# PSUM banks split by user, RWKV operands computed in PSUM, and the recurrence's old state added by products with the identity

## The chip, the cores and the metric

The kernel runs on one core of a Trainium2 chip. The metric is the device time of one execution in microseconds; the median of several runs is compared. The engines are TensorE (PE, with its weight loads PEld), VectorE (DVE), ScalarE (ACT), GpSimd (POOL) and SyncE (SP), which issues the DMAs. PSUM has eight banks of 512 float32 values on 128 partitions.

## The reference

One trunk layer over 256 context tokens and 2048 latent tokens, width 1024. The input is normalised and modulated, then projected once to all the columns that three mixers need: a chunkwise mLSTM (6 heads of 64), an RWKV-7 recurrence (6 heads of 64, two directions) and an RG-LRU (256 channels). The mixers' gated outputs are concatenated and projected back. The part of the reference that the change is about is the RWKV recurrence, one step per token:

```
def rwkv_step(S, inp):
    r, w, kh, b, kt, v = inp
    Sk = einsum('bhvk,bhk->bhv', S, kh)
    S = S * w[:, :, None, :] - Sk[..., None] * b[:, :, None, :] + v[..., None] * kt[:, :, None, :]
    return S, einsum('bhvk,bhk->bhv', S, r)
```

with `w = exp(-DECAY * sigmoid(w0 + tanh(wl) @ w2))` and `b`, `kt` built from `a = sigmoid(a0 + al @ a2)`.

## The kernel before

The kernel is one long program. A planner on the host (class Flow) decides the order of TensorE's instructions alone: processes written as generators issue products and then yield how long they would wait, or an Event; Flow advances a model clock by a cost for each product, serves the process of lowest rank that is ready, and lets the dense projection (rank 9) fill the gaps. Flow knows nothing of PSUM banks. The order on the other engines is chosen by the tile framework, which also inserts the semaphores; `high_priority` pulls an instruction forward there. A PSUM tile is one bank, and a tile that is asked for waits until a bank of its pool is released by its last reader.

The stages, with their time in the trace: modulation and gates (0 to 100 us), the dense projection with the token shift (to 637), **derive** (637 to 1045), the mLSTM (to 1378), and the **chains** (forward to 1729, backward to 2017), with a tail to 2058. The dense projection goes on beside derive and the mLSTM; partial output products (`po`, function out_part) run beside the forward chains, and the final output (`pz`, `yT`, function out_last) beside the backward chains.

PSUM before the change: one pool `ps` of eight banks with one tag, from which every stage and every dense product takes.

**derive** makes the operands of the recurrence, in 54 blocks of 256 tokens (of one head pair `p` and one direction `d`), grouped in seven stages of six or eight blocks. `block()`: four products put the decay and the gate into the bank `pw`; ScalarE's tanh brings both into the SBUF tile `KB` (L950, L952); VectorE makes the sigmoid of the decay (L955) and its running sum (L956, a scan); ScalarE takes two exponentials (E at L957, cs at L958) and one of two scaled gates (L960), VectorE the other (L959); four VectorE products (L965, L967, L969 or L971, L972) make the operands, which DMAs store to DRAM. `worker()`: some 11 us of Flow's time later eight small products fill the bank `pt` from KB, and six ScalarE copies bring its parts to `DG` and `OF` (L1007 to L1009). When all blocks of a stage are there, VectorE transposes DG (L1049) and GpSimd inverts the triangles in 60 small operations (L1058, L1060); `merge()` finishes with products pY and pX.

**chains** runs the recurrence for three head pairs at once, as three processes, each with 36 steps of 64 tokens forward and 36 backward. `prepare` makes the operands of two steps (banks `ga`, `gb`; L1592, L1595, L1598). A step uses one bank `cq`, cut in four parts of 64 columns, `qk`, `yy`, `pp`, `ps`, with a product for each of the two heads on its half of the partitions:

1. `qk` and the first part of `yy` from the old state (eight passes on TensorE, `cq<-cg`; a float32 product is two passes);
2. ScalarE: `q = -qk` (L1630), and GpSimd: `sd` = old state times the decay `Dk` (L1635);
3. `pp` from q; two copies of pp into the place of the state, both on VectorE forward (L1644) or both on ScalarE backward (L1642);
4. `ps` (`cq<-cg,bt`) and the second part of `yy` (`cq<-cg,G`);
5. VectorE, once for each head: new state = ps times Dk plus sd (L1659); yy is copied by ScalarE forward (L1667) or added by VectorE backward (L1665).

A step yields WAIT of 1.38, 0.9 and 1.28 us of Flow's time between its parts, or LONG while the RG-LRU isn't done.

Of the kernel before, what the change touches and what calls it, by code (L numbers as in the profile page):

```python
# [228 lines left out]
def tile_hymba(ctx, tc, I, O):  # L229
# [64 lines left out]
    X["sh_open"] = Event()  # L294
    X["ps"] = ctx.enter_context(tc.tile_pool(name="ps", bufs=8, space=PSUM))
# [16 lines left out]
def side(X, ctx):  # L312

    F, tc = X["F"], X["tc"]
    yield from build_h(X)
    yield X["done"][_GATES]
    with tc.tile_pool(name="gr", bufs=1, side="right") as gr:
        rows = Event()
        F.spawn(gate_rows(X, gr, rows), 2)
        with tc.tile_pool(name="mg", bufs=1, side="right") as mg:  # L320

            gt = [mg.tile([128, T], F32, name=n) for n in ("gt", "RA", "RB")]
            for i, g in enumerate(gt):
                X["nc"].gpsimd.memset(g, 0.0)
                for q in range(4):
                    X["nc"].sync.dma_start(g[32 * q:32 * q + 6], X["U"][_GATES][32 * i + 6 * q:32 * i + 6 * q + 6])
            for g in gt[1:]:
                X["nc"].vector.tensor_tensor(out=gt[0], in0=gt[0], in1=g, op=ALU.add)
            yield 15000.0
            yield from gates(X, mg, *gt)  # L330
        if rows.t is None:
            yield rows
    with tc.tile_pool(name="sh", bufs=1, side="right") as sh:
        shift_setup(X, sh)
        F.fire(X["sh_open"])
        lru_in = Event()
        F.spawn(lru_gates(X, sh, lru_in), 2)
        for n in _SEQ2:
            yield X["done"][n]
            yield from shift_post(X, sh, n)  # L340
            F.fire(X["post"][n], 0.0)
        if lru_in.t is None:
            yield lru_in
# [12 lines left out]
def late(X, ctx):  # L356
# [4 lines left out]
    X["last"], X["parted"] = Event(), Event()  # L361
# [163 lines left out]
def projector(X):  # L525
# [45 lines left out]
    group = [pick(), pick()]  # L571
    with X["tc"].tile_pool(name="w0", bufs=1, side="left") as w0:
# [5 lines left out]
        ps = {(n, b): X["ps"].tile([56 if n == _GATES else 128, 512], F32, tag="b", name=f"pp_{n}_{b}") for n in group for b in (1, 0)}  # L578
# [13 lines left out]
        for b, (t0, n) in list(enumerate(BLOCKS))[2:]:  # L592
            if X["hb"][b].t is None or X["hb"][b].t > F.now:
                yield X["hb"][b]
            ps = X["ps"].tile([56, 512], F32, tag="b", name=f"pp_{_GATES}_{b}")
# [12 lines left out]
            ps = X["ps"].tile([128, 512], F32, tag="b", name=f"pp_{name}_{b}")  # L608
# [5 lines left out]
    while nxt:  # L614
# [8 lines left out]
        for b in (1, 0, 2, 3, 4):  # L623
# [6 lines left out]
            ps = X["ps"].tile([128, 512], F32, tag="b", name=f"pp_{name}_{b}")  # L630
# [202 lines left out]
def derive(X, dv):  # L833
# [13 lines left out]
    Es = []  # L847
    for i in range(2):
        Es.append(dv.tile([128, 4, 65], F32, name=f"E{i}"))
        nc.gpsimd.memset(Es[i][:, :, 0:1], 1.0)  # L850
# [24 lines left out]
    ahead, cnt = [], [0]  # L875
# [21 lines left out]
    def merge(sid, XT, g, end):  # L897
# [4 lines left out]
        pY = X["ps"].tile([128, 16, 32], F32, tag="b", name=f"pY{sid}{g}")  # L902
# [8 lines left out]
        pX = X["ps"].tile([128, 16, 32], F32, tag="b", name=f"pX{sid}{g}")  # L911
# [17 lines left out]
    def block():  # L929

        _, sid, p, d, i0, l0, nm, wa, z = ahead.pop(0)
        E = Es[cnt[0] % 2]
        cnt[0] += 1
        bw = d == 1
        pw = X["ps"].tile([128, 2, 256], F32, tag="b", name=f"pw{nm}")
# [11 lines left out]
        sa = KB[:, :, 0]  # L947
        sw = KB[:, :, 1]
# [15 lines left out]
        k = KB[:, :, 2:4]  # L964
        nc.vector.tensor_tensor(out=k, in0=k, in1=z4, op=ALU.mult)  # L965
        kh, r3 = tok(z[:, 0]), z[:, 1].rearrange("p (c j) -> p c j", j=64)
        nc.vector.tensor_tensor(out=KB[:, :, 1], in0=E[:, :, 0:64], in1=kh, op=ALU.mult)  # L967
        if bw:
            nc.vector.tensor_tensor(out=KB[:, :, 0], in0=E[:, :, 64:0:-1], in1=r3[:, ::-1], op=ALU.mult)  # L969
        else:  # L970
            nc.vector.tensor_tensor(out=KB[:, :, 0], in0=E[:, :, 1:65], in1=r3, op=ALU.mult)  # L971
# [751 lines left out]
def out_part(X, ou, W):  # L1723
# [16 lines left out]
    while nxt:  # L1740
        t, parts = nxt
        o = ou.tile([128, D], F32, tag="o", name=f"o{t}", bufs=3)
        for n in range(2):
# [3 lines left out]
            if n == 0:  # L1747
                nxt = load()
# [222 lines left out]
```

## Time and profile before

| what | value |
| --- | --- |
| median of 3 runs | 2064.82 us (2057.7 to 2073.31) |
| the profiled execution | 2059.59 us |
| its span, first to last instruction | 2057.9 us |
| PE busy over the span | 1801.6 us (88%) |
| DVE, ACT, POOL busy | 1367.0 (66%), 977.6 (48%), 795.0 us (39%) |
| mean granted TensorE clock | 0.933 of full speed |

Busy time is an average over stages with different limits, so it is read stage by stage. The granted clock is the share of full speed that TensorE was given in a stretch. An engine waits in order: what stands behind a waiting instruction waits too.

### The profile page before, as it was taken

The page shows a single profiled execution, that of the slowest core. Times are in us where ns is not written, and L with a number is a line of the kernel's source. Part 1 is how long each engine was busy: PE and PEld are TensorE (multiplying, and loading weights), DVE is VectorE, ACT ScalarE, POOL GpSimd, SP SyncE. Part 2 cuts the span into 40 slices and gives each one's busy share as a digit, 9 for nine tenths or more (in the row PEclk, how much of TensorE's full clock was granted, in tenths as well). Part 3 has the DMA queues.
Part 4 walks back from the last instruction along what each step waited for, and adds up shares of the span by engine and source line. Part 5 has one row for each costly group of instructions (what it writes and reads, how often), then busy time and mean ns, then how long its engine had stood idle before and what let it go on. Part 6 is the DMA issues. An engine that isn't in the chain of part 4 may idle for free. (4 is left out here: it accounts for less than half of the span.)

```text
span 2057.9 us, 46221 instructions
## 1 busy us (share of the span) xinstructions
PE 1801.6 (88%) x16648; PEld 1201.0 (58%) x16778; DVE 1367.0 (66%) x3271; ACT 977.6 (48%) x2634; POOL 795.0 (39%) x1200
## 2 busy tenths in 40 slices
PE   5899999999999878788899798878778788999996
PEld 3555655656666556555566565555555556777774
DVE  3747366777643898998324766647885576777774
ACT  5732446565434667776242545542332233444442
POOL 0210011112110688888722444342653232444442
PEclk9899999999999988889999899989888999999997
DMA  7343344564548778887254666645986545576662
GB/s 284 118 142 90 126 123 133 153 168 148 132 127 247 215 207 223 225 214 176 80 154 135 188 171 170 171 118 154 292 268 193 164 136 149 163 196 203 197 190 72
DMA packets 353370, 350.60 MB, mean 170 GB/s; under 512 B 109554, under 2 KB 294978, under 8 KB 350728
## 3 DMA queue, kind: packets, MB, share of 16 engines
q1 hardware_dynamic: 353142, 347.65, 59.2%
q8 instruction: 133, 2.18, 0.5%
q14 instruction: 95, 0.78, 0.1%
HBM read 211.18 MB, written 136.37 MB: 169 GB/s over the span
## 5 line engine op out<-in xcount | busy, mean ns | idle before, releaser
L1635 POOL TENSOR_SCALAR sd<-cg,Dall 128x128 f32<-128x128 f32 x210 | 135.8, 654 | 267.1 <-DVE cg L1659 164.0
L1659 DVE SCALAR_TENSOR_TENSOR cg<-cq,Dall,sd 64x64 f32<-64x64 f32 x408 | 114.5, 281 | 46.4 <-PE cq L168 36.6
L1060 POOL TENSOR_TENSOR W<-W,tmp 128x30 f32<-128x30 f32 (+14 forms) x210 | 139.0, 662 | 16.1
L1058 POOL TENSOR_TENSOR tmp<-W 128x30 f32<-128x30 f32 (+14 forms) x210 | 133.0, 633 | 15.9
L168 PE MATMUL cq<-cg,bt 128*64 128x64 f32 x840 | 68.5, 246 | 49.7 <-DVE cg L1644 44.6
L1283 ACT ACTIVATE nb<-nb,aT 128x128 f32<-128x128 f32 x216 | 71.6, 393 | 82.5 <-DMA nb<-nm_d 72.4
L168 PE MATMUL cq<-cg 128*64 128x64 f32 x1728 | 92.9, 230 | 8.2 <-DVE cg L1659 8.2
L168 PEld LDWEIGHTS cq<-cg,bt 128*64 128x64 f32 x840 | 44.1, 142 | 84.9 <-DVE cg L1644 54.8
L168 PE MATMUL ga<-cg 64*64 64x128 f32 (+1 forms) x864 | 76.9, 270 | 16.9 <-DMA cg<-ch 16.9
L1630 ACT ACTIVATE q<-cq 128x64 f32<-128x64 f32 x216 | 45.5, 223 | 95.7 <-PE cq L168 92.3
L1592 DVE TENSOR_TENSOR cg<-gb,rmask 64x256 f32<-64x256 f32 x108 | 44.7, 413 | 66.3 <-PE gb L168 61.1
L168 PEld LDWEIGHTS cq<-cg 128*64 128x64 f32 x1728 | 72.9, 141 | 24.3 <-issue 9.5
L168 PE MATMUL pz<-owhi,zhi 128*128 128x512 f32 x180 | 82.1, 456 | 4.5 <-ACT zhi L1822 4.5
L1598 ACT ACTIVATE bt<-ga 128x256 f32<-128x256 f32 x108 | 41.3, 383 | 87.0 <-DVE G L1595 83.4
L168 PE MATMUL pt<-KB 64*64 64x64 f32 x864 | 41.9, 244 | 45.7 <-DVE KB L972 45.6
L1284 POOL TENSOR_SCALAR_AFFINE_SELECT nb<-nb 128x256 f32<-128x256 f32 x108 | 44.8, 421 | 93.0 <-ACT nb L1283 63.6
L168 PE MATMUL gb<-cg 64*64 64x128 f32 (+1 forms) x864 | 75.7, 270 | 0.9 <-DMA cg<-ch 0.9
L168 PE MATMUL pz<-owhi,zlo 128*128 128x512 f32 x180 | 73.5, 409 | 3.3 <-DVE zlo L1823 3.3
L168 PE MATMUL pz<-owlo,zhi 128*128 128x512 f32 x180 | 72.9, 405 | 0.0
L168 PEld LDWEIGHTS ga<-cg 64*64 64x64 f32 x864 | 48.2, 142 | 41.9 <-issue 27.9
L168 PE MATMUL cq<-q,cg 128*64 128x64 f32 x864 | 59.4, 236 | 9.9 <-ACT q L1630 9.9
L168 PE MATMUL pp_v<-hhi,whi_v 128*128 128x512 f32 (+1 forms) x120 | 67.4, 562 | 0.3 <-ACT whi_v L514 0.3
(511 smaller groups left out, 6180.0 us busy)
## 6 DMA issues: line engine op xcount, KB each, us to landing
cg<-ch SPq DMA_DIRECT2D x216, 192.0 KB
wa<-wa SPq DMA_DIRECT2D x54, 256.0 KB
z<-z SPq DMA_DIRECT2D x27, 512.0 KB
ch<-KB SPq DMA_DIRECT2D x108, 128.0 KB
ch<-KB SPq DMA_DIRECT2D x54, 256.0 KB
nb<-nm_d SPq DMA_DIRECT2D x108, 128.0 KB
lr<-L SPq DMA_DIRECT2D x16, 768.0 KB
lL<-lr SPq DMA_DIRECT2D x16, 768.0 KB
```

The lines of the kernel that those rows point to most:

```text
L168: self.nc.tensor.matmul(out, lhsT, rhs, start=start, stop=stop, **kw)
L1058: nc.gpsimd.tensor_tensor(out=tv, in0=W[:, j + 1:32, j:j + 1].to_broadcast([128, m, j]), in1=W[:, j:j + 1, 0:j].to_broadcast([128, m, j]), ...
L1060: nc.gpsimd.tensor_tensor(out=W[:, j + 1:32, 0:j], in0=W[:, j + 1:32, 0:j], in1=tv, op=ALU.add)
L1283: nc.scalar.activation(nb[:, d, j], nb[:, d, j], AF.Exp, bias=aT[:, c, d, 2 * p + j:2 * p + j + 1])
L1284: nc.gpsimd.affine_select(out=nb[:, d], in_=nb[:, d], pattern=[[0, 2], [1 - 2 * d, 128]], base=0, channel_multiplier=-1 + 2 * d, compare_o ...
L1592: nc.vector.tensor_tensor(out=cg[o, :, RK[h]], in0=src[o], in1=mask[o, d].rearrange("p a c -> p (a c)")[:, None].to_broadcast([64, 2, 128] ...
L1598: nc.scalar.activation(bt, ga[:, 1], AF.Copy)
L1630: nc.scalar.activation(q, qk, AF.Copy, scale=-1.0)
L1635: nc.gpsimd.tensor_scalar(sd, cg.rearrange("p (n c) -> p n c", c=64)[:, 0::9], Dk, None, op0=ALU.mult)
L1659: nc.vector.scalar_tensor_tensor(out=nxt[h][b], in0=ps[b], scalar=Dk[b], in1=sd[b, 1 - h], op0=ALU.mult, op1=ALU.add)
```

## The change

Banks: two of the eight (`pd`) serve the dense products alone (`pp_`, `po`, `pz`), the other six serve the stage that runs: six of one kind up to the shift and for the mLSTM; for derive two (`m`, pY and pX), three (`c`, pw and the new kb) and one (`b`, pt); for the chains three (`b`: ga, gb, yT) and three (`c`: cq). `po` and `pz` take one of two slots in Flow first.

derive: the decay's sigmoid and its exponential E stay in pw, the sigmoid's affine step goes to ScalarE, both gates are made by ScalarE into a second bank kb, the four VectorE products read PSUM on one side, and the two OF copies of a block go to VectorE.

chains: GpSimd's sd is gone; two products with the identity add the old state into ps, and the new state is ps times Dk, for one head on ScalarE, for the other on VectorE. The two copies of pp are split the same way.

```diff
-    X["ps"] = ctx.enter_context(tc.tile_pool(name="ps", bufs=8, space=PSUM))
+    X["pd"] = ctx.enter_context(tc.tile_pool(name="pd", bufs=2, space=PSUM))
...
+    with tc.tile_pool(name="psa", bufs=6, space=PSUM) as X["ps"]:
...
-    with tc.tile_pool(name="dv", bufs=1, side="right") as dv:
+    with tc.tile_pool(name="dv", bufs=1, side="right") as dv, tc.tile_pool(name="psb", bufs=1, space=PSUM) as X["ps"]:
         yield from derive(X, dv)
-    with tc.tile_pool(name="ml", bufs=1, side="right") as ml:
+    with tc.tile_pool(name="ml", bufs=1, side="right") as ml, tc.tile_pool(name="psm", bufs=6, space=PSUM) as X["ps"]:
         yield from mlstm(X, ml)
...
+    X["ps"] = ctx.enter_context(tc.tile_pool(name="psr", bufs=3, space=PSUM))
     chains(X, ctx.enter_context(tc.tile_pool(name="rc", bufs=1, side="right")))
...
-        pw = X["ps"].tile([128, 2, 256], F32, tag="b", name=f"pw{nm}")
+        pw = X["ps"].tile([128, 2, 256], F32, tag="c", name=f"pw{nm}", bufs=3)
...
-        nc.scalar.activation(sw, pw[:, 0].rearrange("p (c j) -> p c j", j=64), AF.Tanh, scale=0.5, bias=hv[:, i:i + 1])
+        sw, sa = pw[:, 0], pw[:, 1]
+        nc.scalar.activation(sw, sw, AF.Tanh, scale=0.5, bias=hv[:, i:i + 1])
+        nc.scalar.activation(sw, sw, AF.Copy, scale=0.5, bias=0.5)
...
-        nc.scalar.activation(sa, pw[:, 1].rearrange("p (c j) -> p c j", j=64), AF.Tanh, scale=0.5, bias=hv[:, i:i + 1])
+        nc.scalar.activation(sa, sa, AF.Tanh, scale=0.5, bias=hv[:, i:i + 1])
...
-        nc.vector.tensor_scalar(cs, tok(sw), 0.5, 0.5, op0=ALU.mult, op1=ALU.add)
-        nc.vector.tensor_tensor_scan(out=cf, data0=sm, data1=cf, initial=0.0, op0=ALU.mult, op1=ALU.add)
-        nc.scalar.activation(E[:, :, 1:65], cs, AF.Exp, scale=-DECAY)
-        nc.scalar.activation(cs, cs, AF.Exp, scale=DECAY)
-        nc.vector.tensor_scalar(KB[:, :, 2], tok(sa), ab[:, 0, p:p + 1], ab[:, 1, p:p + 1], op0=ALU.mult, op1=ALU.add)
-        nc.scalar.activation(KB[:, :, 3], tok(sa), AF.Identity, scale=ab[:, 2, p:p + 1], bias=ab[:, 3, p:p + 1])
+        nc.vector.tensor_tensor_scan(out=cf, data0=sm, data1=sw[:, ::-1] if bw else sw, initial=0.0, op0=ALU.mult, op1=ALU.add)
+        k = X["ps"].tile([128, 4, 2, 64], F32, tag="c", name=f"kb{nm}", bufs=3)
+        sat = tok(sa)
+        for s in range(2):
+            nc.scalar.activation(k[:, :, s], sat, AF.Identity, scale=ab[:, 2 * s, p:p + 1], bias=ab[:, 2 * s + 1, p:p + 1])
+        E = sw.rearrange("p (c j) -> p c j", j=64)
+        nc.scalar.activation(sw, cf, AF.Exp, scale=-DECAY)
+        nc.scalar.activation(cf, cf, AF.Exp, scale=DECAY)
...
-        nc.vector.tensor_tensor(out=KB[:, :, 1], in0=E[:, :, 0:64], in1=kh, op=ALU.mult)
+        nc.vector.tensor_copy(KB[:, :, 1, 0:1], kh[:, :, 0:1])
+        nc.vector.tensor_tensor(out=KB[:, :, 1, 1:64], in0=E[:, :, 0:63], in1=kh[:, :, 1:64], op=ALU.mult)
...
-        nc.vector.tensor_tensor(out=k, in0=cs[:, :, None].to_broadcast([128, 4, 2, 64]), in1=k, op=ALU.mult)
+        nc.vector.tensor_tensor(out=KB[:, :, 2:4], in0=cs[:, :, None].to_broadcast([128, 4, 2, 64]), in1=k, op=ALU.mult)
...
-                nc.scalar.activation(OF[sid][a:a + 32, ls], pt[a:a + 32, :, 32:64], AF.Copy)
+                nc.vector.tensor_copy(OF[sid][a:a + 32, ls], pt[a:a + 32, :, 32:64])
...
-    parts, slots, pairs = [0] * NT, Slots(F, 4), Slots(F, NP)
+    parts, slots, pairs = [0] * NT, Slots(F, 3), Slots(F, NP)
...
-                with X["tc"].high_priority(offset=HP):
-                    sd = rc.tile([128, 2, 64], F32, tag="sd", name=f"sd{nm}", bufs=3)
-                    nc.gpsimd.tensor_scalar(sd, cg.rearrange("p (n c) -> p n c", c=64)[:, 0::9], Dk, None, op0=ALU.mult)
+                for h, b, o in heads:
+                    F.mm(ps[b], ident[:, b], cg[:, ST[h]], start=False, stop=False, skip_group_check=True)
...
-                    if d:
+                    if h:
                         nc.scalar.activation(cg[b, ST[h]], pp[b], AF.Copy)
...
-                        nc.vector.scalar_tensor_tensor(out=nxt[h][b], in0=ps[b], scalar=Dk[b], in1=sd[b, 1 - h],
-                                                       op0=ALU.mult, op1=ALU.add)
+                    if not last and h:
+                        nc.vector.tensor_scalar(nxt[h][b], ps[b], Dk[b], None, op0=ALU.mult)
+                    elif not last:
+                        nc.scalar.activation(nxt[h][b], ps[b], AF.Copy, scale=Dk[b])
```

## Rows read from the trace of the kernel before

**Rows 1.** Busy time by stretch: PE, PEld, DVE, ACT, POOL, clock, DMA share, GB/s.
```profile
700.00:950.00 250.00, 202.74 (x2349) 141.44 (x2373) 234.09 (x323) 179.29 (x554) 214.16 (x310) 0.85 0.83 218
1378.00:1729.00 351.00, 278.24 (x3580) 196.53 (x3588) 245.93 (x737) 111.27 (x359) 132.66 (x178) 0.89 0.67 195
1550.00:1729.00 179.00, 145.08 (x2055) 104.70 (x2052) 116.75 (x396) 59.57 (x200) 49.44 (x77) 0.92 0.56 161
1757.00:2017.00 260.00, 253.80 (x3492) 186.26 (x3488) 202.06 (x628) 120.77 (x450) 118.36 (x137) 1.00 0.64 186
```

**Rows 2.** Groups by line, VectorE, 637 to 975 us: count | busy us, mean ns | idle before.
```profile
L972 DVE TENSOR_TENSOR KB<-cs,KB 128x512 f32<-128x512 f32 x54 | 48.2, 898 | 3.2 <-ACT cs L958 3.2
L965 DVE TENSOR_TENSOR KB<-KB,z 128x512 f32<-128x512 f32 x54 | 47.4, 880 | 0.1
L956 DVE TENSOR_TENSOR_SCAN cs<-sm,cs 128x256 f32<-128x256 bf16 x54 | 40.8, 755 | 0.1
L959 DVE TENSOR_SCALAR KB<-KB,rab 128x256 f32<-128x256 f32 x54 | 34.4, 637 | 1.1
L967 DVE TENSOR_TENSOR KB<-E,z 128x256 f32<-128x256 f32 x54 | 33.4, 618 | 5.1 <-ACT E L957 5.0
L955 DVE TENSOR_SCALAR cs<-KB 128x256 f32<-128x256 f32 x54 | 25.3, 469 | 17.6 <-ACT KB L950 17.5
L969 DVE TENSOR_TENSOR KB<-E,z 128x256 f32<-128x256 f32 x27 | 18.9, 701 | 0.0
```

**Rows 3.** Groups by line, ScalarE, 637 to 975 us.
```profile
L960 ACT ACTIVATE KB<-KB,rab 128x256 f32<-128x256 f32 x54 | 32.3, 600 | 0.6
L1008 ACT ACTIVATE OF<-pt 32x128 f32<-32x128 f32 x108 | 27.2, 252 | 0.0
L950 ACT ACTIVATE KB<-pw,hv 128x256 f32<-128x256 f32 x54 | 25.5, 473 | 9.3 <-DMA ch<-KB 8.3
```

**Rows 4.** Single tiles and lines, VectorE: ns min/median/max, first and last start.
```profile
L965 DVE TENSOR_TENSOR KB<-KB,z x54: 658/884/1730, 645.8 to 965.2; 128x512 f32<-128x512 f32 x54
...
L1832 DVE TENSOR_TENSOR zo<-pz,zo x36: 678/681/693, 1764.7 to 2049.1; 128x512 f32<-128x512 f32 x36
...
L1592 DVE TENSOR_TENSOR cg<-gb,rmask x108: 374/417/419, 1379.4 to 2002.2; 64x256 f32<-64x256 f32 x108
...
L1595 DVE TENSOR_TENSOR G<-ga,rmask x108: 282/283/283, 1380.5 to 2003.3; 64x128 f32<-64x128 f32 x108
```

**Rows 5.** Line 1049: the transpose that opens each of derive's seven stages.
```profile
L1049 DVE STREAM_TRANSPOSE W<-DG x7: 1916/1996/2076, 680.1 to 972.3; 128x1024 f32<-128x1024 f32 x7
```

**Rows 6.** Line 1667 (yr<-cq, 108 times): its engine sat idle until: us, times.
```profile
  DVE cg L1659: 75.2, 64
```

**Rows 7.** Timeline of the backward half: start us, us, engine, line, operation.
```profile
1864.10 0.20 PEld L168 LDWEIGHTS cq<-cg,G 128*64 128x64 f32 x4
...
1864.21 0.32 PEld L168 LDWEIGHTS cq<-cg 128*64 128x64 f32 x8
1864.27 0.40 PE L168 MATMUL cq<-cg 128*64 128x64 f32 x8
...
1864.78 0.23 ACT L1630 ACTIVATE q<-cq 128x64 f32<-128x64 f32 x1 [1.63 <-PE cq L168]
```

**Rows 8.** Timeline of the forward half, two places.
```profile
1400.84 0.31 PEld L168 LDWEIGHTS cq<-cg 128*64 128x64 f32 x8 [0.23 <-issue]
...
1401.45 0.22 ACT L1630 ACTIVATE q<-cq 128x64 f32<-128x64 f32 x1
...
1691.34 0.48 DVE L1644 COPY cg<-cq 64x64 f32<-64x64 f32 x2 [0.19 <-PE cq L168]
...
1691.87 0.20 PEld L168 LDWEIGHTS cq<-cg,bt 128*64 128x64 f32 x4 [0.58 <-DVE cg L1644]
```

**Rows 9.** The page's costliest groups: sd on GpSimd, the new state on VectorE.
```profile
L1635 POOL TENSOR_SCALAR sd<-cg,Dall 128x128 f32<-128x128 f32 x210 | 135.8, 654 | 267.1 <-DVE cg L1659 164.0
L1659 DVE SCALAR_TENSOR_TENSOR cg<-cq,Dall,sd 64x64 f32<-64x64 f32 x408 | 114.5, 281 | 46.4 <-PE cq L168 36.6
```

More of the change, by code (lines that the diff above doesn't have):

```diff
@@ L293, in tile_hymba @@
     X["hk"] = [Event() for _ in range(NK)]
-    X["sh_open"] = Event()
-    X["ps"] = ctx.enter_context(tc.tile_pool(name="ps", bufs=8, space=PSUM))
+    X["sh_open"], X["open"] = Event(), Event()
+    X["pd"] = ctx.enter_context(tc.tile_pool(name="pd", bufs=2, space=PSUM))
     with ExitStack() as sa:
@@ L314, in side @@
     F, tc = X["F"], X["tc"]
[L315 to L343, printed above, removed]
-    with tc.tile_pool(name="dv", bufs=1, side="right") as dv:
+    with tc.tile_pool(name="psa", bufs=6, space=PSUM) as X["ps"]:
+        F.fire(X["open"])
+        yield from build_h(X)
+        yield X["done"][_GATES]
+        with tc.tile_pool(name="gr", bufs=1, side="right") as gr:
+            rows = Event()
+            F.spawn(gate_rows(X, gr, rows), 2)
+            with tc.tile_pool(name="mg", bufs=1, side="right") as mg:
+                gt = [mg.tile([128, T], F32, name=n) for n in ("gt", "RA", "RB")]
+                for i, g in enumerate(gt):
+                    X["nc"].gpsimd.memset(g, 0.0)
+                    for q in range(4):
+                        X["nc"].sync.dma_start(g[32 * q:32 * q + 6], X["U"][_GATES][32 * i + 6 * q:32 * i + 6 * q + 6])
+                for g in gt[1:]:
+                    X["nc"].vector.tensor_tensor(out=gt[0], in0=gt[0], in1=g, op=ALU.add)
+                yield 15000.0
+                yield from gates(X, mg, *gt)
+            if rows.t is None:
+                yield rows
+        with tc.tile_pool(name="sh", bufs=1, side="right") as sh:
+            shift_setup(X, sh)
+            F.fire(X["sh_open"])
+            lru_in = Event()
+            F.spawn(lru_gates(X, sh, lru_in), 2)
+            for n in _SEQ2:
+                yield X["done"][n]
+                yield from shift_post(X, sh, n)
+                F.fire(X["post"][n], 0.0)
+            if lru_in.t is None:
+                yield lru_in
@@ L360, in late @@
     X["todo"], X["ahead"] = [1, 0] + list(range(NT - 1, 1, -1)), []
-    X["last"], X["parted"] = Event(), Event()
+    X["last"], X["parted"], X["banks"] = Event(), Event(), Slots(F, 2)
     ou = ctx.enter_context(tc.tile_pool(name="ou", bufs=1, side="left"))
@@ L571, in projector @@
     group = [pick(), pick()]
+    yield X["open"]
     with X["tc"].tile_pool(name="w0", bufs=1, side="left") as w0:
@@ L577, in projector @@
         ev = {n: evac(X, n) for n in group}
-        ps = {(n, b): X["ps"].tile([56 if n == _GATES else 128, 512], F32, tag="b", name=f"pp_{n}_{b}") for n in group for b in (1, 0)}
+        ps = {(n, b): X["pd" if n == _GATES else "ps"].tile([128, 512], F32, tag="b", name=f"pp_{n}_{b}")[0:56 if n == _GATES else 128]
+              for n in group for b in (1, 0)}
         for k in range(NK):
@@ L846, in derive @@
         nc.vector.tensor_scalar(ab[off, 2 * s + 1], ka[off], -0.5, 1.0, op0=ALU.mult, op1=ALU.add)
[L847 to L850, printed above, removed]
     CP = TP // 64
@@ L976, in block @@
         nc.sync.dma_start(ch[64:128, :, 2:4], KB[64:128, :, 0:2])
-        nc.scalar.activation(X["Dall"][:, p, d, i0:i0 + per], E[:, :, 64], AF.Copy)
+        nc.scalar.activation(X["Dall"][:, p, d, i0:i0 + per], E[:, :, 63], AF.Copy)
         if d:
@@ L1743, in out_part @@
         for n in range(2):
-            po = X["ps"].tile([128, 512], F32, tag="b", name=f"po{t}{n}")
+            yield from X["banks"].take()
+            po = X["pd"].tile([128, 512], F32, tag="b", name=f"po{t}{n}")
             yield from out_mm(F, po, n, parts, W)
             nc.scalar.activation(o[:, 512 * n:512 * n + 512], po, AF.Copy)
+            X["banks"].give()
             if n == 0:
@@ L1828, in head @@
             ns = slice(512 * n, 512 * n + 512)
-            po = X["ps"].tile([128, 512], F32, tag="b", name=f"pz{t}{n}")
+            yield from X["banks"].take()
+            po = X["pd"].tile([128, 512], F32, tag="b", name=f"pz{t}{n}")
             yield from out_mm(F, po, n, parts, W)
@@ L1835, in head @@
             nc.scalar.activation(po, o[:, ns], AF.Square, accum_out=ss[:, n:n + 1])
+            X["banks"].give()
         nc.vector.tensor_tensor(out=ss[:, 0:1], in0=ss[:, 0:1], in1=ss[:, 1:2], op=ALU.add)
```

26 lines of the change are left out of this document (10 added, 16 removed).

## The prediction

> **What bounds the kernel now.** I read the windows by stage first, then the groups by line of the stage in question, then the timeline of single steps. Three stages are touched by more than the naming of banks.
>
> The stage that prepares the recurrence's operands (derive) is held by VectorE: in 700 to 950 us it is busy for 234 of 250 us, ScalarE for 179, TensorE for 203 at a granted clock of 0.85 [rows 1]. Its pace is the distance of the seven transposes that open a stage of eight blocks: 972.3 - 680.1 = 292.2 us for six, 48.7 us a stage, 6.09 us a block [rows 5]. VectorE's seven operations of a block add up to 0.90 + 0.88 + 0.76 + 0.64 + 0.62 + 0.47 + 0.70 = 4.96 us [rows 2]; transposes and the rest fill what is left.
>
> The forward half of the chains (1378 to 1729 us) is held by no engine: TensorE works 278 of 351 us, so 73 us are idle, at a clock of 0.89 [rows 1]. The backward half with the final output (1757 to 2017) is held by TensorE: 253.8 of 260 us at a clock of 1.00, 6.2 us idle [rows 1]. What is added to TensorE's queue there lengthens the kernel one for one.
>
> **One property of the waits decides this case.** In a forward step ScalarE's copy of yy (L1667) reads columns 64 to 127 of the bank cq; nothing that it needs comes from VectorE, which reads columns 192 to 255 of the same bank at L1659. Yet 64 of 108 copies waited for L1659, 75.2 us in all [rows 6]. So accesses of two engines to one bank are kept in the order of the program, whichever columns they touch. The change puts new work into exactly such places.
>
> **Part 1, the banks of the dense products.** They get two of their own. A bank is written by 24 products of 512 columns. Four passes of 64 columns take 1864.21 - 1864.10 = 0.11 us [rows 7], 0.028 each, so 24 products last over 24 x 8 x 0.028 = 5.4 us, and emptying one takes 0.68 us on VectorE [rows 4] plus about as much on ScalarE before it. The second bank is free long before it is wanted, and TensorE's order is written by the planner, which knows nothing of banks here. I take 0; the ends are -5 us (waits of products for a bank that a stage held) and +10 us (an emptying that stands behind something else).
>
> **Part 2, derive.** Off VectorE go L955 (0.47) and L959 (0.64). The four products keep one operand in SBUF and get one in PSUM. With two SBUF operands L965 took 658 to 1730 ns, median 884; with one in PSUM a VectorE instruction of the same width took 678 to 693 ns although GpSimd was half busy, and those of 256 and 128 columns were as steady at 0.42 and 0.28 [rows 4]. So: scan 0.76, two products of 512 columns 1.36, two of 256 columns 0.84, a copy of four elements at most 0.24 (half of the two copies of 0.48 [rows 8]; I take 0.2), two OF copies 2 x 0.28 = 0.56: 3.72 us instead of 4.96, 1.24 us a block. If VectorE stayed the bound, 48 blocks would give -60 us.
>
> It does not stay alone. ScalarE gets a copy (0.47 by L950) and a second Identity (0.60 by L960) and gives up two OF copies (0.25 each): +0.57 us a block, 41 blocks in 250 us, so 179 + 23 = 202 of 250 us [rows 1, 3]. And by the property above a block becomes one file of hand-overs: three activations on the bank pw, scan, two Identities, two Exp, products, ScalarE's Dall; and the six copies out of pt, which ran in one engine, alternate ScalarE, VectorE, ScalarE, twice. In series: 3 x 0.47 + 0.76 + 2 x 0.60 + 2 x 0.47 (an Exp by L950) + 0.2 + 2 x 0.42 + 0.68 = 6.0 us, and with some ten hand-overs of 0.11 (1864.67 to 1864.78 [rows 7]) about 7. A block takes two banks of three (pw and kb), so one and a half blocks are under way: 7 / 1.5 = 4.7 us a block at the best, against 6.09 now. I take 5.8, since ScalarE now stops twice a block for a VectorE queue that also holds transposes of 2 us [rows 5]: 48 x 0.3 = -15 us. Ends: -60 (VectorE's relief in full) and +20 (54 blocks that lose 0.4 us each to the stops).
>
> **Part 3, the identity products.** Removed: GpSimd's sd, 210 times 0.65 us, and the two-operand form of 408 VectorE instructions [rows 9]. VectorE's and GpSimd's time was not on the path of the backward half. In each pair of halves one copy moves to the other engine; by the order within a bank they follow one another: 0.24 + 0.11 + 0.22 = 0.57 us instead of 0.48 for pp, and about 0.57 instead of 0.56 for the state. That adds 0.1 us to a step's latency, 36 x 0.1 = 4 us where latency counts (forward).
>
> Added: two products a step, four passes, 0.11 us [rows 7]. And a wait: the identity product writes into cq after q's activation has read qk from cq in the program, so TensorE, which has just issued yy, stops until q is read. Queued behind it on TensorE are the other two chains' products, prepare and all dense work, and every engine that waits for those. Backward: the last eight passes begin to issue at 1864.21 and are out at 1864.44; q ends at 1864.78 + 0.23 = 1865.01; TensorE restarts 0.05 us after a release (copies end at 1691.82, weight load at 1691.87 [rows 8]). The stop is 1865.06 - 1864.44 = 0.62 us [rows 7] with ScalarE free. ScalarE is 46% busy there (120.8 of 260 [rows 1]) with pieces of 0.2 to 0.6 us, so I add 0.1: 0.72. For the 105 steps: 75.6 + 105 x 0.11 = 87 us; up to 6 us of it fall into idle time: **+85** (ends 81 and 87).
>
> Forward: issue ends at 1400.84 + 0.23 = 1401.07, q at 1401.45 + 0.22 = 1401.67, restart 1401.72: 0.65 us [rows 8]. 105 x (0.65 + 0.11) = 80 us, against 73 us of idle time. Part of that idle time is a wait for things that come sooner relative to a later TensorE, part is chain latency that stays. I let half be absorbed: 40 + 4 for latency = **+44** (ends: 80 - 73 = 7, and 110, when nothing is absorbed and q stands behind ScalarE's waits for L1659 of 75.2 / 64 = 1.2 us [rows 6]).
>
> Clock: 81% busy went with 0.92 (1550 to 1729), 98% with 1.00 [rows 1]. The backward half would be busy for (254 + 12) / (260 + 80) = 78%; at 0.92 its 266 us of work would cost 23 us more; I take half, **+12**.
>
> The Trainium skill has a rule on this in "PSUM — Partial Sum Buffer", section "PSUM bank collisions raise a hardware error": two engines on one bank must be kept apart by bank and by group of 32 partitions, whatever the columns. That is the wait of the identity product, whose columns and q's lie on the same 128 partitions, and it speaks against the change; with rows 6 the trace agrees. The same section lets different groups of partitions overlap; by that the two halves of 64 partitions could run side by side, and the forward half would come out some 16 us lower than in my sum. No row shows such an overlap.
>
> **Sum.** The profiled execution took 2059.6 us (the median of the three runs is 2064.8, 0.25% above). 2059.6 - 15 + 0 + 44 + 85 + 12 = 2185.6, so **2186 us**, 6% slower.
>
> **Rivals.** (a) Faster: the identity product does not wait, because the order within a bank is kept between reads but a product into other columns may pass. Then the backward half pays only 105 x 0.11 = 12 us, the forward half hides its 12, and derive keeps three quarters of VectorE's relief, -45: 2059.6 + 12 - 45 = 2027. It holds if TensorE starts the identity product within 0.1 us of yy; against it stands the waiting yr copy. (b) Slower by less: derive gets all of the 60 and the forward half absorbs all it can: 2059.6 - 60 + 7 + 81 = 2088. For it: VectorE's 94%. (c) Slower by more: nothing is absorbed, the clock falls, and derive is stopped by its hand-overs: 2059.6 + 20 + 110 + 87 + 23 = 2300. For it: three engines then wait for one another in each step. (d) Nothing to be measured: q is read sooner, because ScalarE has less in front of it, and a stop costs 0.3 us: backward 105 x 0.41 = 43, forward 0, derive -45: 2058.
>
> **How the numbers follow.** My case 0.56, (a) 0.10, (b) 0.15, (c) 0.13, (d) 0.06. A measurement of this kernel tells about 1% from no change; so faster 0.10, same 0.06, slower 0.84. My case by itself runs from about 2130 to 2240; the range reaches to (b) and (c), 2075 to 2300, and leaves out (a), (d) and half of (c).
>
> **What would show it.** Right: among TensorE's waits a large new one of the product cq<-ident or its weight load for ScalarE's q, over 200 times and 0.5 us or more each, some 130 to 160 us in all; in the backward half TensorE's idle time rises from 6 to over 60 us and the stretch from 288 us (1729 to 2017) to about 385; derive's stages still 44 to 49 us apart, VectorE well under 90% there, ScalarE waiting for OF copies. Wrong: identity products that follow yy at once; a backward half under 310 us; stages of derive under 42 us.

## The result, and the profile after

| | before | after |
| --- | --- | --- |
| median of 4 runs | 2064.24 us | 2271.96 us (2265.87 to 2274.33) |
| ratio | | **1.0998**, interval 1.0951 to 1.1046: slower |
| the profiled execution, its span | 2059.59, 2057.9 us | 2265.87, 2264.2 us |

The stages below are the distances between first starts in the traces: of a product into pw, of pk (the mLSTM's first), of ga, of the 109th q (the first backward step), and of the last q. In the trace after they stand at:

```profile
662.00 0.82 PE L168 MATMUL pw<-wa,w20first 128*128 128x256 f32 x4
...
1123.74 0.49 PE L175 MATMUL pk<-ident,vk 128*128 128x128 f32 x3
...
1850.71 0.23 ACT L1633 ACTIVATE q<-cq 128x64 f32<-128x64 f32 x1 [1.18 <-PE cq L168]
```

| stage | before | after | difference | forecast |
| --- | --- | --- | --- | --- |
| up to derive | 637.7 | 662.0 | +24 | 0 (dense banks) |
| derive | 418.7 | 461.7 | +43 | -15 |
| mLSTM | 321.6 | 324.2 | +3 | |
| forward chains | 349.5 | 402.8 | +53 | +44 |
| backward chains | 290.4 | 374.3 | +84 | +85, and +12 for the clock |
| tail | 40.0 | 39.1 | -1 | |

The sum is +206 us. Two thirds of it lie where the forecast had put nearly all; a third lies in two places to which it had given nothing, or a gain.

TensorE's waits, the view of all waits of the kernel after (engine, product, line, who released it: us in total, times, longest):

```profile
PEld cq L168 <- ACT q L1633: 152.6, 211, 3.3
...
PE cq L168 <- ACT q L1633: 122.2, 210, 3.1
...
PE pt L168 <- ACT DG L1012: 80.9, 33, 8.5
```

The first two lines are the forecast wait, seen from the weight loads and from the products: in all 210 steps the identity products stand for q, the loads 152.6 / 211 = 0.72 us each, the products 122.2 / 210 = 0.58 us. The third line was not forecast. The next that matters is in the list for 300 to 722 us, which ends 60 us into derive:

```profile
PE pp_v L168 <- ACT ug L746: 16.9, 4, 9.0
...
PE pp_k L168 <- ACT ug L746: 3.8, 1, 3.8
```

The windows, in the columns of [rows 1]: derive, the forward half, the backward half.

```profile
722.00:972.00 250.00, 192.74 (x2065) 132.38 (x2085) 160.51 (x324) 181.73 (x498) 166.04 (x314) 0.84 0.76 196
1448.00:1851.00 403.00, 311.58 (x3993) 219.47 (x4000) 187.34 (x526) 161.30 (x571) 60.59 (x70) 0.86 0.59 169
1851.00:2225.00 374.00, 311.46 (x4356) 225.64 (x4358) 217.82 (x698) 143.18 (x499) 65.45 (x48) 0.97 0.50 144
```

In the backward half TensorE is idle for 374 - 311.5 = 62.5 us, where [rows 1] had 6. In derive no engine is nearly full any more: VectorE fell from 234 to 161 of 250 us, and yet its stages stand further apart (before in [rows 5], 48.7 us):

```profile
L1052 DVE STREAM_TRANSPOSE W<-DG x7: 1961/1996/2005, 722.2 to 1048.0; 128x1024 f32<-128x1024 f32 x7
```

(1048.0 - 722.2) / 6 = 54.3 us a stage. The single step, from the timeline of the backward half (as [rows 7]):

```profile
1959.81 0.32 PEld L168 LDWEIGHTS cq<-cg 128*64 128x64 f32 x8
...
1959.87 0.40 PE L168 MATMUL cq<-cg 128*64 128x64 f32 x8
...
1960.43 0.20 ACT L1633 ACTIVATE q<-cq 128x64 f32<-128x64 f32 x1
1960.68 0.20 PEld L168 LDWEIGHTS cq<-cg,ident 128*64 128x64 f32 x4 [0.55 <-ACT q L1633]
1960.68 0.34 PE L168 MATMUL cq<-cg,ident 128*64 128x64 f32 x4 [0.41 <-ACT q L1633]
```

The last weight load of the eight products ends at 1960.13, the products are out at 1960.27, q is read from 1960.43 to 1960.63, and only then does the identity product begin, with everything behind it in TensorE's queue.

### The profile page after: what moved, and what is told of

It is laid out like the page before. It is cut to its first block, busy times and chain, and to the rows that moved or that the text cites. A ratio compares the mean times of both kernels' runs of the same rounds, so it can differ in the third digit from the quotient of the medians.

```text
span 2264.2 us, 47168 instructions
## 1 busy us (share of the span) xinstructions
PE 1893.4 (84%) x17487; PEld 1259.4 (56%) x17618; DVE 1248.6 (55%) x3115; ACT 1072.6 (47%) x2843; POOL 603.0 (27%) x988
## 5 line engine op out<-in xcount | busy, mean ns | idle before, releaser
L168 PE MATMUL cq<-cg,ident 128*64 128x64 f32 x840 | 74.4, 258 | 122.2 <-ACT q L1633 122.2
L168 PEld LDWEIGHTS cq<-cg,ident 128*64 128x64 f32 x840 | 44.1, 143 | 152.3 <-ACT q L1633 152.3
L1664 ACT ACTIVATE cg<-cq,Dall 64x64 f32<-64x64 f32 x204 | 59.3, 309 | 131.3 <-PE cq L168 130.3
L1647 DVE COPY cg<-cq 64x64 f32<-64x64 f32 x216 | 42.1, 210 | 133.2 <-PE cq L168 120.5
L1063 POOL TENSOR_TENSOR W<-W,tmp 128x30 f32<-128x30 f32 (+14 forms) x210 | 109.7, 522 | 16.5
L1061 POOL TENSOR_TENSOR tmp<-W 128x30 f32<-128x30 f32 (+14 forms) x210 | 103.1, 491 | 15.9
L1662 DVE TENSOR_SCALAR cg<-cq,Dall 64x64 f32<-64x64 f32 x204 | 57.3, 290 | 80.9 <-ACT cg L1664 77.1
L168 PEld LDWEIGHTS pt<-KB 64*64 64x64 f32 x864 | 36.1, 161 | 92.0 <-ACT DG L1012 89.3
L1719 POOL TENSOR_TENSOR y<-y 128x384 f32<-128x384 f32 x18 | 20.1, 1116 | 239.3 <-DMA y<-ym 239.3
L1853 POOL TENSOR_TENSOR zo<-zo,zx 128x1024 f32<-128x1024 f32 (+1 forms) x18 | 41.4, 2301 | 141.4 <-DMA cg<-ch 68.5
```

Source lines behind the costliest of these rows:

```text
L168: self.nc.tensor.matmul(out, lhsT, rhs, start=start, stop=stop, **kw)
L1061: nc.gpsimd.tensor_tensor(out=tv, in0=W[:, j + 1:32, j:j + 1].to_broadcast([128, m, j]), in1=W[:, j:j + 1, 0:j].to_broadcast([128, m, j]), ...
L1063: nc.gpsimd.tensor_tensor(out=W[:, j + 1:32, 0:j], in0=W[:, j + 1:32, 0:j], in1=tv, op=ALU.add)
L1647: nc.vector.tensor_copy(cg[b, ST[h]], pp[b])
L1662: nc.vector.tensor_scalar(nxt[h][b], ps[b], Dk[b], None, op0=ALU.mult)
L1664: nc.scalar.activation(nxt[h][b], ps[b], AF.Copy, scale=Dk[b])
```

## The experiments

All ratios are to the kernel before, run on the same chip. Experiments 1 to 4 ask which part costs what, 5 to 8 why derive and the stretch ahead of it grew, 9 to 12 what in derive can be mended.

**1. The identity products ahead of q.** The change, with one statement moved: TensorE's order stays the same, but the identity product no longer follows q in the program.

```diff
+            if not last:
+                for h, b, o in heads:
+                    F.mm(ps[b], ident[:, b], cg[:, ST[h]], start=False, stop=False, skip_group_check=True)
             with X["tc"].high_priority(offset=HP):
                 nc.scalar.activation(q, qk, AF.Copy, scale=-1.0)
-            if not last:
-                for h, b, o in heads:
-                    F.mm(ps[b], ident[:, b], cg[:, ST[h]], start=False, stop=False, skip_group_check=True)
```

> The changed kernel with one edit: the two identity products stand before q's activation in the program instead of behind it; TensorE's own order is the same, so only the wait moves. Theory A (the identity product waits for ScalarE's q because both touch the bank cq): the 122 us that TensorE waited for q at the identity products go; the backward half falls from 374 us to 300 to 315 (before: 290, plus 12 us of products), the forward half from 391 to 345 to 365, the whole from 2266 to about 2150 (2130 to 2170). Theory B (the chains lost to three banks for cq and to copies split over two engines): it stays within 25 us of 2266.

Measured: 2146.83 us, 1.042 (1.0395 to 1.0445). By the ratios that is (1.0998 - 1.042) x 2062 = 119 us less than the kernel after. Forward 337 us, backward 311. TensorE's wait in this run, where after had 122.2 us:

```profile
PE cq L168 <- ACT q L1638: 7.5, 6, 3.4
```

So the wait is the cost of the identity products, and it comes from their place in the program alone. Set beside 3, which has no identity products (1.0391; forward 347.2, backward 298.4), they now neither gain nor lose anything that can be told: the forward half is 10 us shorter, the backward half 13 us longer, near the 105 x 0.11 us that the products themselves take.

**2. The identity part alone**, on the kernel before: the lines of the chains from the change's diff, nothing else.

```diff
-                    nc.gpsimd.tensor_scalar(sd, cg.rearrange("p (n c) -> p n c", c=64)[:, 0::9], Dk, None, op0=ALU.mult)
+                for h, b, o in heads:
+                    F.mm(ps[b], ident[:, b], cg[:, ST[h]], start=False, stop=False, skip_group_check=True)
...
```

> The kernel before with the recurrence's part alone: identity products behind q, copies and states split over ScalarE and VectorE; eight shared banks, derive as before. Theory A: forward and backward half grow as in the changed kernel (338 to about 391, 290 to about 374), the whole is about 2060 + 137 = 2197 (2170 to 2215). Theory B (banks): 2060 to 2090.

Measured: 2180.81 us, 1.0591 (1.0564 to 1.0617); forward 390.2, backward 375.0 us, derive 423.7.

```profile
PE cq L168 <- ACT q L1630: 127.9, 211, 5.4
```

The wait comes with the identity products whichever banks the kernel has.

**3. The other parts alone**: the change without its lines in the chains (sd is back on GpSimd).

> The changed kernel without the recurrence's part: sd on GpSimd, both copies and both states on one engine as before; the split banks and derive as changed. Theory A: the chains are back at 338 and 290 us, the stages up to the mLSTM stay 70 us later (24 in the shift stage, 43 in derive): about 2129 (2115 to 2150). Theory B: the chains stay long, over 2200.

Measured: 2140.04 us, 1.0391 (1.0365 to 1.0416); forward 347.2, backward 298.4 us, derive 464.1, up to derive 667.1. The chains are nearly as before; the loss in derive and ahead of it has nothing to do with them.

**4. The OF copies back on ScalarE.** My first guess for derive: six copies out of pt that alternate between two engines.

```diff
-                nc.vector.tensor_copy(OF[sid][a:a + 32, ls], pt[a:a + 32, :, 32:64])
+                nc.scalar.activation(OF[sid][a:a + 32, ls], pt[a:a + 32, :, 32:64], AF.Copy)
```

> The changed kernel with one edit in derive: the two OF copies of a block back on ScalarE. Theory C (derive lost because the six copies out of pt alternate between two engines, each waiting for the other in its queue): derive falls from 462 to 410 to 430 us, the whole to about 2225. Theory D (derive lost because pt has one bank, whatever engine empties it, and ScalarE gets more work): derive stays at 450 us or more, the whole within 15 us of 2266.

Measured: 2281.57 us, 1.1078 (1.1029 to 1.1127), derive 461.8. The alternation is not it: derive is as long as in the kernel after. TensorE's waits of this run show what happens instead: the time moves from pt's bank to those of pw (7.2 us of such waits in the kernel after).

```profile
PE pw L168 <- DVE KB L975: 54.0, 15, 7.9
PE pt L168 <- ACT DG L1012: 27.2, 16, 4.0
```

**5. Three banks for pt**, shared with pY and pX.

```diff
-            pt = X["ps"].tile([128, 4, 64], F32, tag="b", name=f"pt{nm}", bufs=1)
+            pt = X["ps"].tile([128, 4, 64], F32, tag="m", name=f"pt{nm}", bufs=3)
```

> The changed kernel, but the small products pt of derive take their bank from three that they share with pY and pX, instead of a bank of their own beside two for pY and pX. Profiled after: derive 462 us, TensorE waits 80.9 us for ScalarE's copies out of the one pt bank. Theory D1, the single pt bank holds TensorE, with all that is queued behind it: the wait for the pt bank falls under 30 us, derive takes 420 to 440 us, the kernel 2225 to 2250. Theory D2, the hand-overs inside a block's banks pw and kb and their three banks hold derive whatever pt has: the stop moves to pw, as it did when the OF copies went back to ScalarE, derive stays at 455 to 465 us and the kernel at 2255 to 2275.

Measured: 2270.25 us, 1.1007 (1.0981 to 1.1034), derive 465.3. As theory D2 had it, the pt wait fell to 14.2 us and this took its place:

```profile
PE pw L168 <- DVE KB L975: 62.1, 13, 9.9
```

**6. The shifted tensors' products in the six banks.**

```diff
-            ps = X["pd"].tile([128, 512], F32, tag="b", name=f"pp_{name}_{b}")
+            ps = X["ps" if name in _SEQ2 else "pd"].tile([128, 512], F32, tag="b", name=f"pp_{name}_{b}")
```

> The changed kernel, but the dense products of the tensors that are shifted (r, k, v and the like, evacuated by ScalarE and the shift stage) take their banks from the stage's six, the other dense products keep the two of their own. Theory E1, two dense banks are too few where ScalarE empties them late (TensorE waited 16.9 + 3.8 us for ScalarE in products of v and k): these waits go, what lies ahead of derive falls from 662 to 638 to 645 us, and the kernel takes 2240 to 2252. Theory E2, ScalarE itself is behind in that stretch and the banks only show it: TensorE waits elsewhere, the stretch stays at 655 to 667 us and the kernel at 2258 to 2275.

Measured: 2253.7 us, 1.0928 (1.0905 to 1.0952), by the ratios 14 us less than after, with intervals that just touch, and 2 us above E1's range. The waits for ug are gone from the list, and derive starts at 642.0 us. The stretch goes as theory E1 has it: two dense banks are too few while ScalarE empties them late; that is 20 of the 24 us there.

**7. Derive's five kinds of product share six banks** (one tag with six buffers for pw, kb, pt, pY, pX).

> The changed kernel, but derive's five kinds of product (pw, kb, pt, pY, pX) share six banks in turn instead of 3 + 1 + 2. Theory D3, the division is at fault and six banks are enough: TensorE's waits for ScalarE in pt and pw fall under 25 us in all, derive takes 405 to 430 us, the kernel 2205 to 2235. Theory D4, the chain of hand-overs between ScalarE and VectorE within a block is at fault: derive stays above 445 us and the kernel above 2245, with the stop on whichever bank comes round next.

Measured: 2283.74 us, 1.108 (1.1051 to 1.1109), derive 473.8: 12 us longer than with the banks divided, so that D4 holds. The wait is on the next bank that comes round:

```profile
PE pw L168 <- ACT Dall L980: 36.9, 13, 4.0
```

**8. Derive's chains in PSUM alone**, on the kernel before with its eight shared banks: block() as the change has it, nothing else.

> The kernel before with derive's block alone changed: its chains run in PSUM (pw and kb in the eight shared banks), OF copies stay on ScalarE, no banks of its own for the dense products, no identity products. Theory D3, only the division of the banks made derive slow: derive falls from 419 us to 370 to 400, since VectorE is relieved of 1.2 us a block, and the kernel takes 2015 to 2045, faster than before. Theory D4, hand-overs in a block's banks hold derive: derive takes 430 to 465 us and the kernel 2070 to 2105. Between the two (405 to 425 us, 2045 to 2065): relief and hand-overs cancel.

Measured: 2138.78 us, 1.0364 (1.0339 to 1.0389), derive **493.5**: 75 us more than before, beyond what either theory had said, and 32 more than after. The number of banks is not the cause, and their division even helps. The timeline of one block in this run shows a candidate, which 9 tests (start and duration in us, in brackets the idle time before and who ended it; ScalarE and VectorE alone):

```profile
855.43 0.45 ACT L944 ACTIVATE pw<-pw,hv 128x256 f32<-128x256 f32 x1
...
856.31 0.45 ACT L947 ACTIVATE pw<-pw,hv 128x256 f32<-128x256 f32 x1
...
856.79 0.69 DVE L950 TENSOR_TENSOR_SCAN cs<-sm,pw 128x256 f32<-128x256 bf16 x1 [2.23 <-ACT pw L947]
...
857.51 1.11 ACT L954 ACTIVATE kb<-pw,rab 128x256 f32<-128x256 f32 x2 [0.76 <-DVE cs L950]
...
858.66 0.70 DVE L961 TENSOR_TENSOR kb<-kb,z 128x512 f32<-128x512 f32 x1 [1.18 <-ACT kb L954]
...
859.59 0.41 DVE L966 TENSOR_TENSOR KB<-pw,z 128x256 f32<-128x256 f32 x1
...
860.04 0.17 ACT L974 ACTIVATE Dall<-pw 128x4 f32<-128x4 f32 x1 [0.55 <-DVE KB L966]
```

The two Identities (L954) read a and have no use for the scan (L950), which reads w; but w and a are halves of one bank, so they stand for it, 0.76 us. VectorE stood 2.23 us before the scan and 1.18 before kb. Dall, four elements out of the same bank, stands 0.55 us for VectorE's product, and so does what ScalarE has queued behind it; in 26 of 53 cases that includes the next block's first tanh, in the others the tanh had gone ahead of Dall. This block takes 860.21 - 855.43 = 4.78 us in a file in which mostly one engine works at a time; over all 54 the mean from first tanh to Dall is 6.8 us, and blocks start 7.6 us apart.

**9. w and a in two banks, and Dall from SBUF**, on the kernel of 8.

```diff
-        pw = X["ps"].tile([128, 2, 256], F32, tag="b", name=f"pw{nm}")
+        pw = [X["ps"].tile([128, 256], F32, tag="b", name=f"p{c}{nm}") for c in "wa"]
...
+        nc.scalar.activation(X["Dall"][:, p, d, i0:i0 + per], cs[:, :, 63], AF.Exp, scale=-DECAY)
         nc.scalar.activation(cf, cf, AF.Exp, scale=DECAY)
...
-        nc.scalar.activation(X["Dall"][:, p, d, i0:i0 + per], E[:, :, 63], AF.Copy)
```

> The kernel before with derive's chains in PSUM, as in the run that did that alone (derive 494 us there), but w and a of a block lie in two banks instead of halves of one, and Dall is taken from cs in SBUF, ahead of the second Exp. Theory D5, order within one bank makes the block a single file: ScalarE waits for VectorE's scan before the two Identities (0.76 us a block, 64.5 us in the profile) and for VectorE's products before Dall (0.55 us), with the next block's tanh queued behind. Then both waits go, 54 blocks save 54 x 1.3 = 70 us or nearly, derive takes 415 to 440 us and the kernel 2055 to 2085. Theory D6, the eight shared banks are at fault (dense products and blocks wait for one another's banks): three banks a block instead of two make that worse, derive takes 485 to 520 us and the kernel 2130 to 2165.

Measured: 2095.36 us, 1.0165 (1.0141 to 1.0189), derive 445.4, both just above D5's ranges. ScalarE's waits for VectorE inside a block, over the whole span, first in the kernel of 8, then what stands in their place here:

```profile
ACT kb L954 <- DVE cs L950: 69.2, 51, 16.5
...
ACT Dall L974 <- DVE KB L966: 11.4, 13, 5.0
...
ACT Dall L974 <- DVE KB L968: 7.8, 13, 1.6
```

```profile
ACT pw L956 <- DVE cs L950: 18.3, 10, 4.6
```

88.4 us of waits became 18.3, and derive became 48 us shorter. So the order within a bank is the cause of 48 us, and D6 falls: three banks a block made it better, not worse. How the 48 us divide between the two banks and Dall was not tried, and 27 of the 75 us stay, so the two waits are not all of it.

**10. The division of the banks alone**: the kernel of 3, with derive's block as before, in SBUF.

> The changed kernel's division of the banks, with the recurrence and derive's block as they were before (chains in SBUF, OF copies on ScalarE, sd on GpSimd). Theory B1, the division costs only in the shift stage: ahead of derive 660 to 668 us, derive 412 to 428 us as before, the kernel 2075 to 2095. Theory B2, three banks for pw and one for pt bind derive too: derive 440 to 465 us, the kernel 2100 to 2130.

Measured: 2102.14 us, 1.0202 (1.0175 to 1.0229), just above B1's range: up to derive 662.2 us, derive 425.0, mLSTM 330.4. So the division costs 24 us ahead of derive. The 6 us more in derive are not to be told from nothing, since derive takes 423.7 us in 2, which leaves it as it was; nor are the 9 us in the mLSTM, which takes 324.2 us with the same banks in the kernel after.

**11. The change's division of labour, all operands in SBUF**, on the kernel before.

```diff
-        nc.vector.tensor_scalar(cs, tok(sw), 0.5, 0.5, op0=ALU.mult, op1=ALU.add)
+        nc.scalar.activation(cs, tok(sw), AF.Copy, scale=0.5, bias=0.5)
...
-        nc.vector.tensor_scalar(KB[:, :, 2], tok(sa), ab[:, 0, p:p + 1], ab[:, 1, p:p + 1], op0=ALU.mult, op1=ALU.add)
-        nc.scalar.activation(KB[:, :, 3], tok(sa), AF.Identity, scale=ab[:, 2, p:p + 1], bias=ab[:, 3, p:p + 1])
+        for s in range(2):
+            nc.scalar.activation(KB[:, :, 2 + s], tok(sa), AF.Identity, scale=ab[:, 2 * s, p:p + 1], bias=ab[:, 2 * s + 1, p:p + 1])
```

> The kernel before with the changed kernel's division of labour in derive (the affine of w and both affines of a on ScalarE, VectorE keeps scan and four products), but every operand stays in SBUF. Theory V1, VectorE's relief is worth having when no bank is passed to and fro: VectorE loses 1.1 us of 6.1 a block, derive falls from 419 to 385 to 410 us, the kernel to 2030 to 2055. Theory V2, ScalarE (72% busy before, 0.97 us more a block) takes VectorE's place as the bound: derive 412 to 435 us, the kernel 2055 to 2080.

Measured: 2057.99 us, 0.9971 (0.9949 to 0.9992), derive 421.5: in V2's ranges, though that ScalarE is the bound is not shown by that. GpSimd's waits point elsewhere. In the kernel before, from its first operation on W to its last (684 to 1026 us), they come to 14.6 us, and the largest group is

```profile
POOL W L1050 <- DVE W L1049: 7.3, 5, 2.4
```

In 11 they are 11.3 us from 787 to 1023 us. With so few pauses GpSimd's solve may have set the pace in both kernels, and VectorE's relief then had nothing to shorten. That is read from the waits and not shown by a run.

**12. The same, with kb in PSUM.**

```diff
+        k = X["ps"].tile([128, 4, 2, 64], F32, tag="b", name=f"kb{nm}")
         for s in range(2):
-            nc.scalar.activation(KB[:, :, 2 + s], tok(sa), AF.Identity, scale=ab[:, 2 * s, p:p + 1], bias=ab[:, 2 * s + 1, p:p + 1])
+            nc.scalar.activation(k[:, :, s], tok(sa), AF.Identity, scale=ab[:, 2 * s, p:p + 1], bias=ab[:, 2 * s + 1, p:p + 1])
```

> The run with after's division of labour in SBUF (derive 421 us), with one operand alone in PSUM: kb, written by ScalarE twice in a row and then read and written by VectorE alone, so that the bank is handed over once a block. Theory G, in the kernel before GpSimd's solve of W held derive (it runs without a pause from one stage to the next, 46 to 53 us a stage, slowed by VectorE's products of two SBUF operands), and in the changed kernel the single file of hand-overs in a block's banks does: with the two largest products off SBUF the solve falls to 37 to 43 us a stage, blocks keep up, six stages take 265 to 288 us instead of 292 to 299, derive 390 to 412 us, the kernel 2028 to 2050, faster than both. Theory H, ScalarE (82% busy in the run it is built on) or the dense products between the blocks hold the stages at 49 us whatever the solve takes: six stages 292 to 305 us, derive 415 to 430, the kernel 2052 to 2072, though the solve is shorter.

Measured: 2069.01 us, 1.0034 (1.0015 to 1.0053), derive 430.8. The same window of derive as in [rows 1], in the kernel of 11 and in this one:

```profile
700.00:950.00 250.00, 193.69 (x2249) 134.91 (x2272) 191.59 (x236) 204.59 (x619) 204.91 (x311) 0.84 0.80 208
```

```profile
700.00:950.00 250.00, 196.63 (x2245) 133.10 (x2243) 156.16 (x224) 200.23 (x607) 175.12 (x305) 0.86 0.78 206
```

VectorE is busy for 234 us before, 192 in 11 and 156 in 12; GpSimd for 214, 205 and 175. The stages did not come closer: this run's seven transposes stand 300.0 us apart from first to last, and 292.2 in [rows 5].

```profile
L1049 DVE STREAM_TRANSPOSE W<-DG x7: 1995/2026/2080, 690.6 to 990.6; 128x1024 f32<-128x1024 f32 x7
```

Theory G falls with this, and H is what came out (derive 0.8 us above its range). Relief of VectorE (11), and of VectorE and GpSimd's solve together (12), shortened nothing; both kernels give ScalarE more to do (179, then 205 and 200 of 250 us), and 12 adds a bank that is handed over. So the solve may still have held derive in the kernel before; what the run shows is that something else holds the stages at nearly the same pace once the solve is shorter. GpSimd now waits, for 57.5 us from its first operation on W (694 us) to its last (1036). No engine is busy for more than 80% in 12 (ScalarE, 200 of 250 us); what holds its stages was not settled.

**What the runs add up to.** Ratios from one step to the next, times 2062 us: the division of banks 0.0202, **+42 us** (10); derive's chains in PSUM on top 1.0391 - 1.0202, **+39** (3 less 10); the identity products on top 1.0998 - 1.0391, **+125** (after less 3). The 75 us of 8 in derive, step by step: the division of labour +3 (11), kb in PSUM +9 (12), w and a in PSUM in two banks +15 (9), in one bank with Dall read from it +48 (8). Each is the difference of two traces, and with derive unchanged two traces differed by 5 us (418.7 and 423.7), so only the larger steps count. Only the kernel of 11 is faster than before, by 0.3%, below the 1% that a measurement tells from no change; it has none of the three parts in it.

## Why the prediction was right, and where it was not

**The wait of the identity product: right.** The forecast was over 200 waits of 0.5 us or more, 130 to 160 us in all, reckoned from the end of the weight loads' issue. So reckoned there are 211 of 0.72 us, 152.6 in all (by the products, which are counted busy a little longer, 210 of 0.58 us and 122.2), and experiment 1 takes them away by the order of the program alone. The property read from [rows 6], that the accesses of two engines to one bank keep the order of the program whichever columns they touch, decided the case, and 48 us of derive in the kernel of 8 as well. Rivals (a) and (d) needed waits of 0.1 or 0.3 us and fall.

**Backward +85: measured +84.** The weight loads' waits for q in the two halves of the kernel after, backward first:

```profile
PEld cq L168 <- ACT q L1633: 70.1, 104, 2.4
```

```profile
PEld cq L168 <- ACT q L1633: 82.5, 107, 3.3
```

70.1 us and 105 x 0.11 for the products make 82, and experiment 2, whose banks are as before, has the half at 375.0 us too. TensorE has 62.5 us of idle time, as "over 60" had it; over the whole half it had 290.4 - 276.0 = 14.4 before, not only the 6 of [rows 1]:

```profile
1727.50:2017.90 290.40, 276.02 (x3937) 203.60 (x3939) 222.60 (x703) 133.30 (x503) 127.47 (x151) 0.98 0.64 184
```

The clock term (+12) was wrong: the granted clock is 0.97 at 311.5 / 374 = 83% busy, where the step "81% busy went with 0.92" had been read from the forward half.

**Forward +44: measured +53**, between the ends. The stop was sized too short: 82.5 / 107 = 0.77 us, where the sum had 0.65. With the products that is 94 us and the 4 for latency 98; 53 came out, so that 45 were absorbed, about half, as the sum had chosen without a row for it. The granted clock fell from 0.89 to 0.86 in this half, for which the sum had no term; what that cost is not shown. The copies and the scaled states of the two heads follow one another, as forecast from the order within a bank:

```profile
DVE cg L1662 <- ACT cg L1664: 77.1, 75, 3.2
...
ACT cg L1645 <- DVE cg L1647: 53.3, 58, 4.2
```

The Trainium skill, "PSUM — Partial Sum Buffer", section "PSUM bank collisions raise a hardware error", would let different groups of partitions of a bank overlap. The two halves here are such groups, and the program nevertheless keeps them apart; that the chip would let them overlap no run here shows.

**Derive -15: measured +43, outside the ends of -60 and +20.** The durations held: a product with an operand in PSUM was forecast at 0.68 us and took 697 and 679 ns, the scan 685. Two other steps failed. First, "its pace is held by VectorE": taken down to 192 and then 156 of 250 us (11, 12), VectorE freed nothing, so neither the end of -60 nor the chosen -15 found a gain there. Second, "one and a half blocks are under way". In the trace after a block lasts 7.6 us from its first tanh to its Dall, near the 7 of the sum, but the blocks start 6.8 us apart: 1.1 are under way, fewer than the banks would allow. What keeps them apart is shown in part: in the kernel of 8, undoing the order within the banks gave back 48 of 75 us (9). In the kernel after the same was not tried, and there 41 of 53 first tanhs start before the Dall of the block ahead of them, so Dall alone does not explain it.

One gain did come that the sum did not have. GpSimd's solve ran faster, since VectorE's products no longer have two SBUF operands; its additions before and after:

```profile
L1060 POOL TENSOR_TENSOR W<-W,tmp 128x30 f32<-128x30 f32 (+14 forms) x210 | 139.0, 662 | 16.1
```

```profile
L1063 POOL TENSOR_TENSOR W<-W,tmp 128x30 f32<-128x30 f32 (+14 forms) x210 | 109.7, 522 | 16.5
```

The Trainium skill, "SBUF — State Buffer", section "Who interferes with whom", says that a VectorE instruction with two SBUF inputs and a GpSimd instruction that reads SBUF share a port and block one another. The traces agree: 662 ns before and 641 in 11, with two SBUF operands; 566 in 12, with one of them in PSUM in the two largest products; 520 in 8 and 522 after, with one in PSUM in all four. It bought nothing, because the blocks were late by then: from GpSimd's first operation on W to its last it now waits for 97 us, where it had waited for 14.6.

**Dense banks 0: measured +24.** The step was "the second bank is free long before it is wanted", with 0.68 us of emptying on VectorE "plus about as much on ScalarE". TensorE waited for the emptying of v's and k's banks by ScalarE (ug, L746), up to 9.0 us at a time. In that longest case ScalarE was not at other work; its read of the bank just ahead of ug had itself stood for a DMA:

```profile
582.34 0.69 ACT L738 ACTIVATE ub_v<-pp_v,mus 128x512 f32<-128x512 f32 x1 [10.87 <-DMA z<-nv]
```

ScalarE stands as long (10.86 us) in experiment 6, where TensorE no longer waits for it: six banks hid that, two did not. The end of "+10 us (an emptying that stands behind something else)" had the mechanism and was too small.

**The total.** 2186 forecast, 2272 measured, 2266 in the profiled execution: direction and main mechanism right, the size short by 80 us in that execution. Derive is 58 of them, the dense banks 24, the forward half 9, and the clock takes 12 off. Rival (c), which let derive lose 20, came closest (2300), but by luck in part: it has 110 us for the forward half and 23 for the clock, where 53 us were measured and, in the backward half, a clock of 0.97.

## What to carry to other kernels

In these kernels the order within a PSUM bank is the order of the program, for reads as for writes and whatever the columns: put an instruction of another engine on the bank ahead of the readers it does not depend on, and give values that two engines handle a bank each. Before an operand is moved into PSUM to relieve an engine, count what each engine's queue holds behind its last access to that bank. And a busy share of 94% is not a price: only a run that relieves the engine, best without loading another, shows whether it held the stage.

## What was not expected of the hardware

The granted clock does not follow from the busy share alone. Before, it was 0.85 in derive and 0.92 late in the forward half, with TensorE 81% busy in both (203 of 250 and 145 of 179 us [rows 1]). In derive of the kernel of 8 it was 0.77 at 185 of 250 us,

```profile
700.00:950.00 250.00, 184.51 (x1837) 123.47 (x1856) 123.17 (x222) 177.78 (x514) 140.07 (x270) 0.77 0.68 173
```

and in the backward half after it stayed at 0.97 at 83%, with 104 short stops for q. And VectorE products with one operand moved to PSUM came back as faster GpSimd additions (662 to 522 ns), although none of the solve's instructions was touched.
